# Sparse attention with two heads' transposes in one stage and one product tile, a planner clock that counts matmuls as traced, and a gate product moved by one place

## The chip, the core and the metric

The kernel runs on one core of one Trainium2 chip. The metric is device time in microseconds, the median of several runs of the same program. A core has a matrix engine (PE, TensorE), a vector engine (DVE), a scalar engine (ACT), GpSimd (POOL) and a queue processor (SP) that issues the memory transfers. Each engine executes its instructions in the order of the program, and semaphores tie the engines together.

## What is computed

Two blocks of a network are run, one behind the other, on 512 tokens of 1024 channels. The first has two layers. Each layer multiplies a normed x by a wide input matrix and feeds three mixers: an mLSTM (`ya`), sparse attention (`yb`) and differential attention (`yc`). Gates weigh the three results, an output matrix follows, and a gated feed-forward part ends the layer. The second block has an even layer (pooling and a spatial gate) and an odd layer (dilated attention and a gated convolution). The change lies in sparse attention, which per query takes the 128 best keys of an indexer:

```python
s = jnp.einsum('bqhd,bqkhd->bhqk', qb, k_sel).astype(f32) * (dh ** -0.5)
s = jnp.where(valid[:, None], s, -jnp.inf)
p = jax.nn.softmax(s, axis=-1).astype(v.dtype)
return jnp.einsum('bhqk,bqkhd->bqhd', p, v_sel)
...
merged = (gates[:, :, 0] * jnp.einsum('btc,cd->btd', y_a, w_branch[0])
          + gates[:, :, 1] * jnp.einsum('btc,cd->btd', y_b, w_branch[1])
          + gates[:, :, 2] * jnp.einsum('btc,cd->btd', y_c, w_branch[2]))
```

## The kernel before

**Tiling.** Tokens are four tiles of 128. A weight GEMM (`gemm`, line 352) accumulates products of 128x128 by up to 512 columns in PSUM tiles named `g`. Every f32 operand is split into two fp32r parts (`whi`, `wlo` of a weight on ACT and DVE; `xh`, `xl` of x), and three products stand for one. In the mixing part of a layer the weight GEMMs run in the order of the table `MIXING` (line 36): projections by name, `("gate", branch, half)` for gate products, `("br", b)` for branch products.

**Sparse attention** (`dsa`) is done by pair of heads (four pairs) and query tile i (four), 16 stages a layer. In the kernel before a stage computes the scores of both heads (`two_scores`: three matmuls a head, each on 64 rows of PE), takes softmax (DVE adds the bias and takes the maximum, ACT exponentiates), and then, head by head, transposes the probabilities (`probs_T`: matmuls against `ident` into a PSUM tile `t`, an ACT copy to `pt`), multiplies them by v into a `t` tile of its own, and scales the product into `y` on ACT. When a pair is through, `pair_over` stores y to the scratch `scr`. When all pairs are through, `load_y` fetches the pairs from `scr` to `tmp` and transposes them for the branch product `("br", 1)`, the last of a layer. The other two mixers do the same for their branches.

**The order of the work** is set while the program is written. The GEMM loop emits one k-step at a time and then calls `advance`, which lets waiting generators ("streams") emit their next step. Each keeps a time at which its inputs will be there. The time comes from a planner's clock: `count` (line 187) adds a cost per instruction to the clock of its engine, and the PE's clock is `now`. A transfer is counted as its bytes plus `LOAD`, 2100 ns. Buffers are counted too (`take`, `give`: two `pt`, two `t`, one set `yT` for the reload). The order on the chip is then fixed; what the planner counted wrongly turns into waits there. All instructions go through a wrapper and so carry line 62 in the profile; they are told apart by the names of their tiles.

**What the prediction touches**: `MIXING` (36), `LOAD` (45), the costs in `count` (187 to 216), `two_scores` (638), `probs_T` (657), `load_y` (668), `dsa` (721), and in `diff` the call of `probs_T`.

Of the kernel before, what the change touches and what calls it, by code (L numbers as in the profile page):

```python
# [10 lines left out]
FR = mybir.dt.float32r  # L11
AF = mybir.ActivationFunctionType
# [3 lines left out]
P = 128  # L16
# [16 lines left out]
POOLS = (2, 4, 8, 16)  # L33


MIXING = ("dq", "dv", "dk", "mo", "mq", "mv", ("gate", 2, 0), "mk", ("gate", 2, 1), "sk", "sv", "sq",
          ("gate", 0, 0), ("gate", 0, 1), ("br", 2), ("gate", 1, 0), ("br", 0), ("gate", 1, 1), ("br", 1))
BRANCHES = [item[1] for item in MIXING if item[0] == "br"]
FREE = "free"
# [84 lines left out]
class Net:  # L124
# [62 lines left out]
    def count(self, name, op, args):  # L187

        s = self.cur
        if name == "sync":  # L190
            self.t[name] = max(self.t[name], self.now) + 4 * math.prod(args[0].shape) / 360.0
            self.arrive = self.t[name] + LOAD
            if s:
                s.ready = max(s.ready, self.arrive)
            return
        n = max(math.prod(a.shape[1:]) for a in args if hasattr(a, "shape"))
        if op == "transpose":
            cost = 107.0
        elif name == "tensor":
            n = math.prod(args[0].shape[1:])  # L200
            cost = max(107.0, n / 2.4 + 3 if args[1].dtype == FR else 4 * n / 2.4)
        else:
            cost = {"vector": (60 + n) / 0.96, "scalar": (200 + n) / 1.4,
                    "gpsimd": 100.0 + n * (200 if op == "tensor_tensor" else 1)}[name]
        start = max(self.t[name], self.now)
        if s and s.last[0] not in (None, name) and op != "memset":
            start = max(start, s.last[1] + 60)
        self.t[name] = start + cost
        if s and op != "memset":
            s.last = (name, start + cost)  # L210
            s.ready = max(s.ready, start + cost + LAG)
        if name == "tensor":
            self.now = self.t[name]
# [206 lines left out]
    def rstd(self, ss, n, count):  # L420
        nc = self.nc
        ms = self.small(n)
        nc.vector.tensor_scalar(ms, ss, 1.0 / count, EPS, op0=OP.mult, op1=OP.add)
        r = self.small(n)
        nc.gpsimd.tensor_tensor(r, ms, self.nhalf[:, :n], op=OP.pow)
        return r
# [211 lines left out]
    def two_scores(self, w, qs, ks, i):  # L638

        ps = self.ps("s"), self.ps("s")  # L640
        ts = slice(i * P, (i + 1) * P)
        for n, (a, b) in enumerate(((0, 0), (0, 1), (1, 0))):
            for c in range(2):
                hp = slice(c * 64, c * 64 + 64)
                self.nc.tensor.matmul(ps[c][:, :w], qs[hp, a, ts], ks[hp, b, :w], start=(n == 0), stop=(n == 2))
        return ps

    def softmax(self, ps, w, bias, scale, total):
# [5 lines left out]
        nc.scalar.activation(s[:, :w], s[:, :w], AF.Exp, bias=m, scale=-1.0, accum_out=total)  # L654
        return s

    def probs_T(self, p, w):

        yield from self.take(pt=1, t=1)
        tr = self.transposed([p[:, j * P:(j + 1) * P] for j in range(w // P)])  # L660
        self.give("s")
        pt = self.buf("pt")
        self.nc.scalar.copy(pt[:, :w], tr[:, :w])
        self.give("t")
        yield
        return pt

    def load_y(self, scr, yT, pair):
# [52 lines left out]
    def dsa(self, q, k, v, bias, out):  # L721
        nc = self.nc
        heads = {}

        def part(pair, i):
            while pair not in heads:
                yield
            qs, ks, vn, y = heads[pair]
            w = (i + 1) * P
            yield from self.take(s=2, S=2)  # L730
            tot = self.small(2)
            pr = []
            for c, ps in enumerate(self.two_scores(w, qs, ks, i)):
                pr.append(self.softmax(ps, w, bias[i], 0.125, tot[:, c:c + 1]))
                self.give("S")
            yield
            r = self.small(2)
            nc.vector.reciprocal(r, tot)
            for c, p in enumerate(pr):
                hp = slice(c * 64, c * 64 + 64)  # L740
                pt = yield from self.probs_T(p, w)
                yield from self.take(t=1)
                yp = self.ps("t")
                for j in range(i + 1):
                    nc.tensor.matmul(yp[:, :64], pt[:, j * P:(j + 1) * P], vn[:, j, hp], start=(j == 0), stop=(j == i))
                self.give("pt")
                nc.scalar.activation(y[:, i, hp], yp[:, :64], AF.Copy, scale=r[:, c:c + 1])
                self.give("t")
                if c == 0:
                    yield  # L750
            if i == NT - 1:
                yield from self.pair_over(y, out, pair)

        yield from self.attend(lambda pair: self.pair_setup(heads, pair, q, k, v),
                               lambda pair: [part(pair, i) for i in range(NT)], 4)

    def attend(self, setup, parts, width):
# [9 lines left out]
    def diff(self, q, k, v, lamn, gout, out):  # L767
        nc = self.nc
        heads = {}

        def part(h, i):
            while h not in heads:
                yield
            qs, ks, vn, y = heads[h]
            w = (i + 1) * P
            yield from self.take(s=2, S=2)
            tot = self.small(2)
            pr = []
            for c, ps in enumerate(self.two_scores(w, qs, ks, i)):
                pr.append(self.softmax(ps, w, self.master[:, T - w:], 0.125, tot[:, c:c + 1]))  # L780
                self.give("S")
            yield
            r = self.small(2)
            nc.vector.reciprocal(r, tot)
            kap = self.small(1)
            nc.vector.tensor_scalar(kap, r[:, 1:2], tot[:, 0:1], lamn, op0=OP.mult, op1=OP.mult)
            nc.vector.scalar_tensor_tensor(pr[0][:, :w], pr[1][:, :w], kap, pr[0][:, :w], op0=OP.mult, op1=OP.add)
            self.give("s")
            yield
            pt = yield from self.probs_T(pr[0], w)  # L790
            yield from self.take(t=1)
            yp = self.ps("t")
            for j in range(i + 1):
                nc.tensor.matmul(yp[:, :P], pt[:, j * P:(j + 1) * P], vn[:, j, :], start=(j == 0), stop=(j == i))
            self.give("pt")
            nc.scalar.activation(y[:, i, :], yp[:, :P], AF.Copy, scale=r[:, 0:1])
            self.give("t")
            sq = self.buf("sq", (P, P))
            ss = self.small(1)
            nc.scalar.activation(sq, y[:, i, :], AF.Square, accum_out=ss)  # L800
            yield
            rr = self.rstd(ss, 1, P)
            yield
            nc.vector.scalar_tensor_tensor(y[:, i, :], y[:, i, :], rr, gout, op0=OP.mult, op1=OP.mult)
            if i == NT - 1:
                yield from self.pair_over(y, out, h)

        yield from self.attend(lambda h: self.pair_setup(heads, h, q, k, v),
                               lambda h: [part(h, i) for i in range(NT)], 4)


# [271 lines left out]
    def plan(self):  # L1083

        ins, want = self.ins, self.want
        for li in range(2):
# [4 lines left out]
            cols = {"dq": C_DQ, "dk": C_DK, "dv": C_DV, "mq": C_MQK, "mk": C_MQK + T, "mv": C_MV, "mo": C_MO, "sq": C_SQ}  # L1091
            for item in MIXING:
                if item in cols:
# [106 lines left out]
    def layer(self, li):  # L1200
# [152 lines left out]
        gates = {}  # L1353
        for item in MIXING:
            if item != "dq":
# [539 lines left out]
```

## Time and profile before

| | us |
|---|---|
| median of 3 runs | 3027.21 (3025.52 to 3029.02) |
| the profiled execution | 3023.1 |
| its span, first to last instruction | 3021.4 |
| PE busy | 2975.6 (98%) |
| DVE busy | 1572.8 (52%) |
| ACT busy | 1163.4 (39%) |
| POOL busy | 115.7 (4%) |

The profile's page gives busy time by engine, the chain of work that ended last, and the costliest groups of instructions. Other views of the same trace give each instruction in order of time, what an engine waited for, and the clock that was granted to PE. A matmul's record is longer than the distance to the next one, because matmuls are pipelined: distances are read from start times. A product in f32 makes two records, a transpose one.

### The profile page before, as it was taken

The page shows a single profiled execution, that of the slowest core. Times are in us where ns is not written, and L with a number is a line of the kernel's source. Part 1 is how long each engine was busy: PE and PEld are TensorE (multiplying, and loading weights), DVE is VectorE, ACT ScalarE, POOL GpSimd, SP SyncE. Part 2 cuts the span into 40 slices and gives each one's busy share as a digit, 9 for nine tenths or more (in the row PEclk, how much of TensorE's full clock was granted, in tenths as well). Part 3 has the DMA queues.
Part 4 walks back from the last instruction along what each step waited for, and adds up shares of the span by engine and source line. Part 5 has one row for each costly group of instructions (what it writes and reads, how often), then busy time and mean ns, then how long its engine had stood idle before and what let it go on. Part 6 is the DMA issues. An engine that isn't in the chain of part 4 may idle for free.

```text
span 3021.4 us, 38554 instructions
## 1 busy us (share of the span) xinstructions
PE 2975.6 (98%) x14474; PEld 2464.4 (82%) x14474; DVE 1572.8 (52%) x3018; ACT 1163.4 (39%) x2176; POOL 115.7 (4%) x128
## 2 busy tenths in 40 slices
PE   8999999999999999999999999999999999999999
PEld 6877887887888788888788888888888888888887
DVE  6888754544435788964444333444652233433534
ACT  4365454332323346545332223322333234444322
POOL 1100100000000110100000000000000000000000
PEclk9999999999999999999999999999999999999999
DMA  4545554535344344664434344424254433443534
GB/s 140 162 133 166 183 176 137 164 98 161 113 140 144 119 137 139 200 199 142 152 128 125 125 140 132 138 93 153 84 168 149 143 104 108 110 114 105 174 109 146
DMA packets 336023, 419.60 MB, mean 139 GB/s; under 512 B 37660, under 2 KB 167132, under 8 KB 335836
## 3 DMA queue, kind: packets, MB, share of 16 engines
q1 hardware_dynamic: 335836, 417.13, 44.0%
q8 instruction: 114, 1.87, 0.3%
q14 instruction: 73, 0.60, 0.1%
HBM read 339.37 MB, written 77.68 MB: 138 GB/s over the span
## 4 chain that ended last, share of the span: by engine, by line
PE 93%; DVE 3%; DMA 2%; ACT 1%; SPq 1%; issue 1%; POOL 0%; DVEq 0%; ACTq 0%; POOLq 0%
PE g L62 83%; PE t L62 6%; PE s L62 3%; DVE tmp L62 1%; DVE wlo L62 1%; SPq L62 1%; DMA wraw<-in_w_in_dram 1%; DVE small L62 0%; ACT whi L62 0%; DMA tmp<-scr 0%; DMA wraw<-in_w_gate_up_dram 0%; DMA scr<-tmp 0%; DMA pt<-in_norm_mix_g_dram 0%; DMA ld<-scr 0%; ACT tmp L62 0%
## 5 line engine op out<-in xcount | busy, mean ns | idle before, releaser
L62 DVE TENSOR_TENSOR wlo<-wraw,whi 128x1024 fp32r<-128x1024 f32 (+1 forms) x502 | 592.2, 1184 | 771.8 <-ACT whi L62 763.3
L62 PE MATMUL g<-xh,whi 128*128 128x512 f32 (+2 forms) x2256 | 889.1, 394 | 0.0
L62 PE MATMUL g<-xh,wlo 128*128 128x512 f32 (+2 forms) x2256 | 866.6, 384 | 0.0
L62 PE MATMUL g<-xl,whi 128*128 128x512 f32 (+2 forms) x2256 | 865.2, 383 | 0.0
L62 ACT ACTIVATE whi<-wraw 128x1024 fp32r<-128x1024 f32 (+1 forms) x502 | 513.5, 1027 | 802.7 <-PE g L62 686.4
L62 PEld LDWEIGHTS g<-xh,wlo 128*128 128x128 f32 (+1 forms) x2256 | 423.3, 188 | 86.1
L62 PEld LDWEIGHTS g<-xh,whi 128*128 128x128 f32 (+1 forms) x2256 | 423.8, 188 | 83.6 <-issue 6.1
L62 PEld LDWEIGHTS g<-xl,whi 128*128 128x128 f32 (+1 forms) x2256 | 424.3, 188 | 74.9
L62 PE MATMUL g<-whi,s 128*128 128x512 f32 x1536 | 480.0, 390 | 3.4 <-ACT tmp L62 3.4
L62 PEld LDWEIGHTS g<-whi,s 128*128 128x128 f32 x1536 | 288.4, 188 | 63.9 <-ACT tmp L62 4.5
L62 PE MATMUL g<-wlo,s 128*128 128x512 f32 x768 | 298.8, 389 | 0.0
L62 PE MATMUL g<-whi,xh 128*128 128x512 f32 x704 | 281.3, 400 | 0.0
L62 PE MATMUL g<-whi,xl 128*128 128x512 f32 x704 | 275.3, 391 | 0.6 <-DVE xl L62 0.6
L62 PE MATMUL g<-wlo,xh 128*128 128x512 f32 x704 | 275.3, 391 | 0.6 <-DVE wlo L62 0.6
L62 POOL TENSOR_TENSOR small<-small,nhalf 128x1 f32<-128x1 f32 (+2 forms) x108 | 110.1, 1021 | 2813.8 <-DVE small L62 2792.4
L62 PEld LDWEIGHTS g<-wlo,s 128*128 128x128 f32 x768 | 144.3, 188 | 29.3
L62 PEld LDWEIGHTS g<-whi,xh 128*128 128x128 f32 x704 | 132.7, 189 | 31.3 <-issue 3.7
L62 PEld LDWEIGHTS g<-whi,xl 128*128 128x128 f32 x704 | 132.6, 188 | 29.7 <-DVE xl L62 1.4
L62 PEld LDWEIGHTS g<-wlo,xh 128*128 128x128 f32 x704 | 132.9, 189 | 26.4 <-DVE wlo L62 1.0
L62 PE MATMUL g<-s,whi 128*128 128x512 f32 x416 | 135.6, 408 | 0.0
L62 ACT ACTIVATE tmp<-g 128x512 f32<-128x512 f32 (+1 forms) x108 | 62.9, 582 | 157.0 <-PE g L62 143.5
L62 DVE SCALAR_TENSOR_TENSOR tmp<-tmp,g 128x512 f32<-128x512 f32 x92 | 63.0, 685 | 97.2 <-ACT tmp L62 85.5
(199 smaller groups left out, 2594.3 us busy)
## 6 DMA issues: line engine op xcount, KB each, us to landing
wraw<-in_w_in_dram SPq DMA_DIRECT2D x120, 512.0 KB, 4.1
wraw<-in_w_gate_up_dram SPq DMA_DIRECT2D x88, 512.0 KB, 4.6
scr<-tmp SPq DMA_DIRECT2D x168, 256.0 KB, 2.8
wraw<-in_odd_w_in_dram SPq DMA_DIRECT2D x64, 512.0 KB, 3.7
ld<-scr SPq DMA_DIRECT2D x104, 256.0 KB, 5.4
wraw<-in_odd_w_in_dram SPq DMA_DIRECT2D x192, 128.0 KB, 2.3
wraw<-in_w_down_dram SPq DMA_DIRECT2D x44, 512.0 KB, 3.8
tmp<-scr SPq DMA_DIRECT2D x80, 256.0 KB, 5.2
```

The lines of the kernel that those rows point to most:

```text
L62: return f(*a, **kw)
```

## The change

- In `dsa` a stage transposes the probabilities of both heads (it takes both `pt` buffers for it), then, one step later, multiplies both and scales both. Both products go to halves of one PSUM tile, `yp[:, hp]`, where each had a tile of its own.
- `probs_T` becomes `transpose_probs`, without the step behind it and without taking `pt`; differential attention calls it with both written out, so that its stages are as before.
- The planner's cost of an fp32r product of n columns goes from n / 2.4 + 3 to (n + 32) / 2.4 ns (512 columns: 216.3 to 226.7), of an f32 product from 4n / 2.4 to no less than 214 ns (64 columns: 107 to 214). Of the two heads' score matmuls only the first is counted.
- In `MIXING` the gate product `("gate", 2, 1)` stands behind `sk` instead of ahead of it.

```diff
-MIXING = ("dq", "dv", "dk", "mo", "mq", "mv", ("gate", 2, 0), "mk", ("gate", 2, 1), "sk", "sv", "sq",
+MIXING = ("dq", "dv", "dk", "mo", "mq", "mv", ("gate", 2, 0), "mk", "sk", ("gate", 2, 1), "sv", "sq",
...
-            cost = max(107.0, n / 2.4 + 3 if args[1].dtype == FR else 4 * n / 2.4)
+            cost = max(110.0, (n + 32) / 2.4) if args[1].dtype == FR else max(214.0, 4 * n / 2.4)
...
-                self.nc.tensor.matmul(ps[c][:, :w], qs[hp, a, ts], ks[hp, b, :w], start=(n == 0), stop=(n == 2))
+                eng = self.nc.tensor if c == 0 else self.nc.tensor.eng
+                eng.matmul(ps[c][:, :w], qs[hp, a, ts], ks[hp, b, :w], start=(n == 0), stop=(n == 2))
...
-    def probs_T(self, p, w):
-
-        yield from self.take(pt=1, t=1)
+    def transpose_probs(self, p, w):
+
+        yield from self.take(t=1)
...
         self.give("t")
-        yield
         return pt
...
-            for c, p in enumerate(pr):
+            yield from self.take(pt=2)
+            pts = []
+            for p in pr:
+                pts.append((yield from self.transpose_probs(p, w)))
+            yield
+            yield from self.take(t=1)
+            yp = self.ps("t")
+            for c, pt in enumerate(pts):
                 hp = slice(c * 64, c * 64 + 64)
-                pt = yield from self.probs_T(p, w)
-                yield from self.take(t=1)
-                yp = self.ps("t")
                 for j in range(i + 1):
-                    nc.tensor.matmul(yp[:, :64], pt[:, j * P:(j + 1) * P], vn[:, j, hp], start=(j == 0), stop=(j == i))
+                    nc.tensor.matmul(yp[:, hp], pt[:, j * P:(j + 1) * P], vn[:, j, hp], start=(j == 0), stop=(j == i))
                 self.give("pt")
-                nc.scalar.activation(y[:, i, hp], yp[:, :64], AF.Copy, scale=r[:, c:c + 1])
-                self.give("t")
-                if c == 0:
-                    yield
+                nc.scalar.activation(y[:, i, hp], yp[:, hp], AF.Copy, scale=r[:, c:c + 1])
+            self.give("t")
...
-            pt = yield from self.probs_T(pr[0], w)
+            yield from self.take(pt=1)
+            pt = yield from self.transpose_probs(pr[0], w)
+            yield
```

PE has 13896 matmuls in both programs. The first place is PE in sparse attention of layer 0, last pair of heads, near its end. `s_` are probabilities, `pt_` their transposes, `ld_` v, `t_` PSUM tiles, `g_` a weight product; the numbers name single buffers, and in brackets stand the semaphores (by producer) that a row waits for. Before, with head 1 of query tile 2 and head 0 of tile 3:

```order
L62 MATMUL t_1355_5347<-ident_87,s_1328_5240 128x128 [waits Activation_49]
L62 MATMUL t_1355_5347<-ident_87,s_1328_5240 128x128 x2
L62 MATMUL t_1357_5353<-ident_87,s_1341_5286 128x128 [waits Activation_49]
L62 MATMUL t_1357_5353<-ident_87,s_1341_5286 128x128 x3
L62 MATMUL g_1293_5131<-xh_94,whi_1290_5118 128x512
L62 MATMUL g_1293_5131<-xl_95,whi_1290_5118 128x512
L62 MATMUL g_1293_5131<-xh_94,wlo_1291_5119 128x512
L62 MATMUL t_1359_5363<-ld_1260_4998,pt_1356_5351 128x64 [waits Activation_49]
L62 MATMUL t_1359_5363<-ld_1260_4998,pt_1356_5351 128x64 x2
L62 MATMUL t_1360_5368<-ld_1260_4998,pt_1358_5358 128x64 [waits Activation_49]
L62 MATMUL t_1360_5368<-ld_1260_4998,pt_1358_5358 128x64 x3
L62 MATMUL g_1317_5208<-xh_94,whi_1286_5102 128x512
```

And in the changed program, both heads of query tile 2:

```order
L62 MATMUL t_1308_5127<-ident_87,s_1289_5063 128x128 [waits PE_49]
L62 MATMUL t_1308_5127<-ident_87,s_1289_5063 128x128 x2
L62 MATMUL t_1310_5133<-ident_87,s_1291_5067 128x128 [waits Activation_49]
L62 MATMUL t_1310_5133<-ident_87,s_1291_5067 128x128 x2
L62 MATMUL g_1299_5091<-s4_1160_4595,whi_1213_4785 128x512
L62 MATMUL g_1299_5091<-s4_1161_4596,whi_1213_4785 128x512
L62 MATMUL g_1299_5091<-s4_1160_4595,wlo_1214_4786 128x512
L62 MATMUL t_1313_5144<-ld_1198_4730,pt_1309_5131 128x64 [waits Activation_49]
L62 MATMUL t_1313_5144<-ld_1198_4730,pt_1309_5131 128x64 x2
L62 MATMUL t_1313_5144<-ld_1198_4730,pt_1311_5137 128x64 [waits Activation_49]
L62 MATMUL t_1313_5144<-ld_1198_4730,pt_1311_5137 128x64 x2
L62 MATMUL g_1314_5153<-s4_1158_4593,whi_1211_4772 128x512
```

The two products that follow each other wrote two tiles (`t_1359`, `t_1360`) and now write one (`t_1313`); the GEMM around them was a gate product (`xh` by weights) and is now the branch product of the mLSTM (`s4` by weights).

The second place is PE where the output of sparse attention comes back (`tmp`, four pairs of heads) and is transposed. Before:

```order
L62 MATMUL g_1332_5257<-xh_94,wlo_1291_5119 128x512
L62 MATMUL t_1379_5441<-ident_87,tmp_1376_5435 128x128 x4
L62 MATMUL t_1381_5450<-ident_87,tmp_1377_5437 128x128 x4
L62 MATMUL t_1383_5459<-ident_87,tmp_1380_5448 128x128 x4
L62 MATMUL t_1384_5466<-ident_87,tmp_1382_5457 128x128 x4
L62 MATMUL g_1385_5473<-s4_1372_5431,whi_1345_5300 128x512
```

In the changed program, the first two of the four:

```order
L62 MATMUL g_1345_5315<-xh_94,wlo_1321_5191 128x512
L62 MATMUL t_1346_5322<-ident_87,tmp_1342_5300 128x128 x4
L62 MATMUL g_1345_5315<-xh_94,whi_1323_5205 128x512
L62 MATMUL g_1345_5315<-xl_95,whi_1323_5205 128x512
L62 MATMUL g_1345_5315<-xh_94,wlo_1324_5206 128x512
L62 MATMUL g_1345_5315<-xh_94,whi_1323_5205 128x512
L62 MATMUL g_1345_5315<-xl_95,whi_1323_5205 128x512
L62 MATMUL g_1345_5315<-xh_94,wlo_1324_5206 128x512
L62 MATMUL t_1348_5337<-ident_87,tmp_1344_5307 128x128 x4
L62 MATMUL g_1349_5344<-xh_94,whi_1320_5190 128x512
```

The transposes stood between the last gate product and the branch product; they now stand among the products of the last gate GEMM, 30 products behind the end of the branch product before it.

## Rows read from the trace of the kernel before

**Rows 1.** The page: busy time by engine, and the chain's shares by engine.

```profile
PE 2975.6 (98%) x14474; PEld 2464.4 (82%) x14474; DVE 1572.8 (52%) x3018; ACT 1163.4 (39%) x2176; POOL 115.7 (4%) x128
...
PE 93%; DVE 3%; DMA 2%; ACT 1%; SPq 1%; issue 1%; POOL 0%; DVEq 0%; ACTq 0%; POOLq 0%
```

**Rows 2.** Timeline in a gate GEMM: start us, us, engine, line, operation, out<-in, shape, count.

```profile
416.03 0.39 PE L62 MATMUL g<-xl,whi 128*128 128x512 f32 x1
...
416.26 0.40 PE L62 MATMUL g<-xh,wlo 128*128 128x512 f32 x1
```

**Rows 3.** What PE waited for: us in total, times, longest us.

```profile
PE t L62 <- DMA tmp<-scr: 14.5, 4, 6.0
...
PE g L62 <- ACT tmp L62: 3.4, 3, 1.7
PE t L62 <- DVE small L62: 2.4, 2, 1.7
...
PE s L62 <- ACT y L62: 0.5, 2, 0.3
```

**Rows 4.** Chain, ends of sparse attention, layers 0 and 1: start, us, what.

```profile
516.94 3.52 PE g L62 x15
...
531.62 3.43 PE g L62 x13
...
1463.26 3.52 PE g L62 x15
...
1477.92 6.21 PE g L62 x20
```

**Rows 5.** Timeline at the end of sparse attention, layer 0; idle before in brackets.

```profile
510.39 0.93 PE L62 MATMUL t<-ident,s 128*128 128x128 f32 x7
...
511.07 0.47 PE L62 MATMUL g<-xh,whi 128*128 128x512 f32 x1
...
522.06 1.06 SPq L62 DMA_DIRECT2D tmp<-scr  x2
...
526.34 1.99 PE L62 MATMUL t<-ident,tmp 128*128 128x128 f32 x8 [5.91 <-DMA tmp<-scr]
```

**Rows 6.** Windows: length, busy us by engine (count), granted clock share, DMA share, GB/s.

```profile
320.00:331.00 11.00, 9.27 (x41) 7.36 (x41) 8.76 (x27) 7.56 (x16) 2.64 (x2) 0.84 0.57 182
394.00:400.00 6.00, 5.75 (x37) 4.78 (x37) 2.77 (x11) 3.13 (x14) 0.00 (x0) 1.00 0.14 50
...
526.00:532.00 6.00, 4.32 (x18) 3.56 (x19) 1.95 (x3) 2.14 (x4) 0.00 (x0) 0.50 1.07 355
...
1472.00:1478.00 6.00, 3.99 (x17) 3.35 (x18) 1.66 (x3) 1.84 (x4) 0.00 (x0) 0.50 1.10 347
```

**Rows 7.** Timeline, products of two heads in a row, layer 0.

```profile
508.57 1.22 PE L62 MATMUL t<-ld,pt 128*128 128x64 f32 x10
```

**Rows 8.** Groups by shape: count, busy us, mean ns, idle before and releasers.

```profile
L62 ACT ACTIVATE whi<-wraw 128x1024 fp32r<-128x1024 f32 x432 | 455.2, 1058 | 711.6 <-PE g L62 599.4 <-DMA wraw<-in_w_gate_up_dram 42.3 <-DMA wraw<-in_w_in_dram 22.5
...
L62 ACT ACTIVATE y<-t,small 128x64 f32<-128x64 f32 x64 | 19.6, 312 | 31.4 <-PE t L62 30.4
```

**Rows 9.** Timeline around one product of sparse attention, layer 0.

```profile
410.00 0.37 ACT L62 COPY pt<-t 128x256 f32<-128x256 f32 x1 [0.71 <-PE t L62]
...
410.45 0.64 PE L62 MATMUL t<-ld,pt 128*128 128x64 f32 x4
...
410.93 0.50 PE L62 MATMUL t<-ident,s 128*128 128x128 f32 x3
411.13 0.31 ACT L62 ACTIVATE y<-t,small 128x64 f32<-128x64 f32 x1 [0.75 <-PE t L62]
```

**Rows 10.** The page's DMA issues: count, KB each, median us to landing.

```profile
tmp<-scr SPq DMA_DIRECT2D x80, 256.0 KB, 5.2
```

**Rows 11.** Timeline of PE, two stops in the mLSTM, layer 0.

```profile
323.18 0.39 PE L62 MATMUL t<-small,last 128*128 128x8 f32 x2 [1.71 <-DVE small L62]
...
395.55 0.62 PE L62 MATMUL s<-s,s 64*128 64x256 f32 x5 [0.26 <-ACT y L62]
```

## The prediction

> **What bounds the kernel now.** I read the page first. TensorE (PE) is busy for 98% of the span, 93% of the chain that ended last lies on it, and no other engine is busy for more than 52% [rows 1]. The 512-column products of the weight GEMMs ("g") start every 0.23 us (416.03, 416.26 [rows 2]). They, the transposes and the attention products fill PE, so an edit counts only if it changes the stops between PE's instructions or their spacing.
>
> Then PE's waits [rows 3]. They are few. The largest item is 14.5 us for `tmp<-scr`, four stops, at the two places where sparse attention ends: PE runs out of GEMM work, and the output of sparse attention has still to come back from memory before it can be transposed for the last branch product.
>
> The chain view shows the whole price [rows 4]. In layer 0 the last fifteen products that cover it end at 516.94 + 3.52 = 520.46, and the branch product starts at 531.62, 11.16 us later. The sixteen transposes between are needed anyway. At 0.10 us each (seven from 510.39 to 511.07 [rows 5]) they are 1.6 us, so 9.5 are lost. In layer 1 it is 1463.26 + 3.52 = 1466.78 to 1477.92, 11.14, so 9.5 again. Behind both stops PE stays slow for a while: the granted clock is 0.50 (1.2 GHz) from 526 to 532 and from 1472 to 1478 [rows 6]. The twenty products from 1477.92 take 6.21 us where 20 x 0.23 = 4.6 would do, the thirteen from 531.62 take 3.43 for 3.0 [rows 4]: 2.0 us more. Together 21.0 us.
>
> **The change part by part.** No instruction is added or removed. What changes is their order, and one dependency.
>
> *One product tile for two heads.* Before, each head's product had a tile of its own, and two heads that met ran without a stop: ten records in a row [rows 7], with ACT scaling behind them. Now both heads write halves of one tile, head 1's product stands straight behind head 0's, and its first matmul waits for ACT: the scaling of head 0, which reads that tile, has to come between. It is so in all 32 stages (4 pairs x 4 query blocks x 2 layers; 64 scalings of 128x64 [rows 8]). PE executes in order, so the GEMM products behind wait too. The price of a turn from one stretch [rows 9]: a product ends at 410.45 + 0.64 = 411.09, ACT starts at 411.13 and takes 0.31, to 411.44; from an ACT end (410.00 + 0.37 = 410.37) to the product that waited for it (410.45) pass 0.08, so PE goes on at 411.52. Without the wait its next work began at 410.93. That is 0.59 us a turn, 32 x 0.59 = **+18.9 us**. Ends: 0.43 (411.09 to 411.52, if the overlap with the product's own end were not lost), 13.8 us; and 0.8 if ACT is met in a 1.06-us weight conversion [rows 8] as often as its busy share of 39% says (0.39 x 0.53 = 0.2 more), 25.6 us. I take 0.59, since ACT's rows ahead of a scaling are the two copies, which end earlier.
>
> The Trainium skill (PSUM — Partial Sum Buffer, section "PSUM bank collisions raise a hardware error") asks that two engines be kept apart by bank and partition quadrant, not by address: disjoint columns don't help, and the new wait is what it asks for. No run here shows the contrary. If columns were enough, this term would be 0 and the sum 18.9 us lower.
>
> *Two transposes per stage.* The copies of both heads now follow each other on ACT, ahead of the products. Three GEMM products (0.7 us) lie between, as before; one copy took 0.37 us for 256 columns [rows 9]. The second copy has head 0's product and the turn as further cover. I take +1 us in all (0 to +4, an eighth of a microsecond a stage).
>
> *The program's clock, and the moved gate product.* The planner counts 226.7 ns for a 512-column product instead of 216.3, as the trace has it, and only one of the two score matmuls that start together. Sparse attention ends earlier against the GEMMs: its last product stands within branch 0, and 96 gate products follow before branch 1, with the reload's transposes among them. From the end of branch 0, which frees the tiles they go to, 30 products (6.8 us) cover what takes 1.6 us to issue (520.46 to 522.06) and 4.3 us more until the transposes start (526.34) [rows 4, 5]. The other three loads have more. So the 21.0 us go but for about 0.7 a layer: **-19.6 us**. The least is -12, if the loads land late behind the weight loads in SP's queue and each layer still waits 4.5 us.
>
> *The other reloads.* Branches 2 and 0 fetch theirs in the same way, and the planner counts 2.1 us for any load (LOAD = 2100), where `tmp<-scr` takes 5.2 us to land [rows 10]. Before, PE waited for none of them: all four stops are at the end. With a shorter cover a stop of up to 3.1 us is possible at the first load of each, four places. I take 1.25 at each, **+5 us** (0 to +12).
>
> *All other re-weaving.* Every step is placed a twentieth fewer products behind what it waits for (216.3/226.7), in differential attention, the mLSTM, the odd layer and at the GEMMs' PSUM tiles. Where cover was just enough PE stops now. Before, such stops cost 3.4 + 2.4 + 0.5 = 6.3 us [rows 3]; they can vanish or double, -6 to +6, and I take **+4**, since covers shrink everywhere. The moved gate product is in this term: it and `sk` change places whole, with their loads.
>
> Sum: 18.9 + 1 - 19.6 + 5 + 4 = **+9.3 us** on the profiled run's 3023.1 us, 3032.4. The median of the runs is 4.1 us above the profiled one: 3027.2 + 9.3 = **3036**.
>
> **Rivals**, as medians; 0.2% (6 us) is about what a measurement of this kernel tells from no change.
>
> *Gain and loss cancel.* The turns cost their lower end and re-weaving nothing: 13.8 + 1 - 19.6 + 5 = 0, 3027. For: the two large terms are of one size and opposite sign. Against: 0.59 is read off neighbouring rows. 28%.
>
> *Faster.* The turn is covered, because head 1's product would have waited for its own copy anyway, and only what exceeds that wait counts. At 0.1 us a turn: 3.2 + 1 - 19.6 + 5 + 4 = -6.4, 3021; the sign turns at 0.30. For: both copies go through ACT, one behind the other. Against: three GEMM products and head 0's product lie between. 5%.
>
> *The clock falls.* Behind a stop of 1.71 us at 323.18 [rows 11] the granted clock was 0.84 over 11 us [rows 6], 0.16 x 11 = 1.8 us lost. If each turn lost half of this, 32 x 0.9 = 29 us: 3065. Against: in 394 to 400, with a short stop at 395.55 [rows 11], the clock stayed at 1.00 [rows 6]. 5%.
>
> The Trainium skill (TensorE: Matmul & The Clock Gate, section "A second HAM failure mode: psum-queue depth-cycling") tells of a kernel in which short idle times at each change of PSUM buffer made the clock fall and rise again. Here the short stop left it at full speed, which is why I give the case no more.
>
> *ACT in the way.* If a weight conversion stands ahead of head 0's scaling in every third turn: 11 x 1.06 = 12 us more, 3048. 10%.
>
> *The tail stays.* If SP's queue holds the reloads back behind weight loads, a stop of 4.5 us a layer stays: 8 us more, 3044. 5%.
>
> **How the numbers follow.** The forecast of +9 has 47%; its own range is +3 to +15 (3030 to 3042), from the bounds of the re-weaving. The rivals take 28, 5, 5, 10 and 5%. The range that should hold the time 8 times in 10 reaches down to the case in which gain and loss cancel (3026) and up to the busy ACT (3048); it leaves out the fallen clock, the faster case and an edge of the cancelling one. Slower by over 0.2%: 0.66 (46 of the forecast's 47, and the three costly rivals' 20); within 0.2%: 0.28; faster: 0.06, the faster rival and one part in a hundred of the forecast.
>
> **What would show it.** Right: PE's waits list about 32 stops at product tiles with ACT `y` as releaser, each about 0.3 us of idle as that view counts; no 6-us stop for `tmp<-scr`; a granted clock above 0.9 behind the end of sparse attention. Wrong: no such stops (the turn is covered), a stop at the end of sparse attention as before, or a granted clock under 0.9 within it. If the stops are there and the time is the same, the re-weaving gave back what I took it to cost.

## The result and the profile after

The changed kernel takes 3046.68 us (median of 4, 3045.11 to 3048.88) against 3026.36 for the kernel before (4 runs): 1.0069 times the time, 95% interval 1.0052 to 1.0087, or 20 us more. The forecast was slower by 9, 3036, in a range of 3026 to 3048. Side and range held; the size was less than half of what came.

The page of the changed kernel gives the span and the busy times, as [rows 1] do for the kernel before:

```profile
span 3047.1 us, 38595 instructions
PE 2989.6 (98%) x14474; PEld 2463.3 (81%) x14474; DVE 1575.2 (52%) x3018; ACT 1163.1 (38%) x2176; POOL 121.2 (4%) x128
```

Work and shares are nearly the same; the span is 25.7 us longer than the profiled one before, where the medians differ by 20. The two profiled executions lie towards opposite ends of their runs (3023.1 us before, 3048.88 now), so some 5 us in what follows are spread between runs. What PE waited for in the changed kernel (us in total, times, longest), as [rows 3]:

```profile
PE t L62 <- DVE tmp L62: 16.2, 11, 11.8
PE t L62 <- ACT y L62: 13.7, 32, 0.8
PE g L62 <- ACT tmp L62: 5.2, 4, 2.2
PE g L62 <- DVE wlo L62: 3.9, 2, 2.8
PE t L62 <- DMA tmp<-scr: 3.6, 2, 3.1
...
PE t L62 <- ACT pt L62: 0.9, 3, 0.3
```

There are 32 stops of a product on ACT `y`, one a stage. The stops at `tmp<-scr` fell from 14.5 us in four to 3.6 in two: the longer (3.1) is at a reload ahead of sparse attention, the other (0.5) at its end in layer 1. And the waits of the GEMMs for ACT `tmp` and DVE `wlo` grew from 4.0 us (3.4 and 0.6) to 9.1. One turn in the timeline (start us, us, engine, line, operation, out<-in, shape, count, idle before in brackets):

```profile
401.84 0.55 PE L62 MATMUL t<-ld,pt 128*128 128x64 f32 x4
...
402.43 0.31 ACT L62 ACTIVATE y<-t,small 128x64 f32<-128x64 f32 x1 [0.61 <-PE t L62]
...
402.80 0.66 PE L62 MATMUL t<-ld,pt 128*128 128x64 f32 x4 [0.41 <-ACT y L62]
```

Head 0's product ends at 402.39, ACT scales it from 402.43 to 402.74, head 1's product starts at 402.80. Windows of the changed kernel (columns as in [rows 6]), the first over sparse attention, the others where the kernel before had just stopped:

```profile
400.00:450.00 50.00, 46.04 (x280) 37.26 (x278) 20.75 (x54) 23.82 (x61) 0.00 (x0) 1.00 0.48 144
526.00:532.00 6.00, 6.00 (x32) 5.02 (x31) 3.83 (x4) 2.93 (x5) 0.00 (x0) 1.00 0.48 156
1472.00:1478.00 6.00, 6.00 (x28) 4.98 (x27) 3.81 (x6) 2.12 (x2) 0.00 (x0) 1.00 0.02 6
```

PE is busy throughout the last two at a granted clock of 1.00, where [rows 6] have 0.50. So both large terms of the sum are there. What is new is in the middle of the mixing part, ahead of sparse attention. PE in layer 0, and below it what DVE did until then:

```profile
290.23 0.50 PE L62 MATMUL g<-xh,wlo 128*128 128x512 f32 x1 [2.81 <-DVE wlo L62]
```

```profile
286.90 1.42 DVE L62 TENSOR_TENSOR tmp<-tmp,lay 128x512 f32<-128x512 f32 x2
288.35 0.69 DVE L62 TENSOR_TENSOR tmp<-tmp,tmp 128x512 f32<-128x512 f32 x1
288.95 1.22 DVE L62 TENSOR_TENSOR wlo<-wraw,whi 128x1024 fp32r<-128x1024 f32 x1
```

DVE works without a pause on normalisations; the part of a weight that PE needs next stands behind them. This one stop comes with the moved gate product and not with the new costs: gate_moved_only and no_clock, below, have a stop of 2.8 us for `wlo` in each layer under the planner's old costs. Other stops of the changed kernel are not in those two, among them the two longest of layer 1:

```profile
1236.95 0.79 PE L62 MATMUL g<-xh,whi 128*128 128x512 f32 x1 [2.23 <-ACT tmp L62]
...
1265.29 1.09 PE L62 MATMUL t<-ident,tmp 128*128 128x128 f32 x4 [3.11 <-DMA tmp<-scr]
```

At all three the granted clock falls to 0.50 for a few microseconds, as these windows of the changed kernel show. The kernel before has one such fall ahead of sparse attention, behind its stop at 323 us [rows 6]:

```profile
290.00:300.00 10.00, 9.77 (x36) 7.92 (x37) 9.30 (x18) 3.12 (x4) 0.00 (x0) 0.83 0.83 259
1230.00:1245.00 15.00, 12.11 (x47) 9.38 (x46) 14.65 (x28) 7.44 (x13) 4.95 (x3) 0.89 0.63 206
1260.00:1275.00 15.00, 11.89 (x50) 9.80 (x49) 7.10 (x20) 7.38 (x17) 0.00 (x0) 0.77 0.85 284
```

Counted as in the prediction, 0.17 x 10 + 0.11 x 15 + 0.23 x 15 = 6.8 us are lost so, where the kernel before loses 1.8. By this estimate 5 us of the loss ahead of sparse attention are the clock.

**Where the time is.** To add it up I took, for each PE record, the distance from its start to the next start, less the usual distance of that kind of record (the lower quartile over all records of that kind in both traces). This excess is summed over three stretches, cut at the same amount of work in every kernel: both layers between the early projections and sparse attention (123 to 386 and 977 to 1334 us in the kernel before), sparse attention with its end (386 to 547, 1334 to 1501), and the rest. Turns are products that stand over 0.4 us too far behind another product.

| kernel | ahead of sparse attention | sparse attention and end | of it turns | rest | sum |
|---|---|---|---|---|---|
| before | 49.3 | 52.7 | 0 | 35.2 | 137.2 |
| changed | 71.2 | 49.3 | 18.9 (32) | 42.6 | 163.1 |
| both_first | 69.2 | 33.1 | 0 | 39.4 | 141.6 |
| heads_only | 50.9 | 54.1 | 19.1 (32) | 35.8 | 140.8 |
| clock_only | 67.7 | 32.5 | 0 | 39.5 | 139.7 |
| fp32r_cost_only | 66.6 | 32.1 | 0 | 40.8 | 139.5 |
| gate_moved_only | 50.9 | 49.1 | 0 | 33.8 | 133.8 |
| no_clock | 51.4 | 52.9 | 19.7 (32) | 36.9 | 141.1 |
| gate_back | 67.9 | 53.0 | 19.3 (32) | 39.5 | 160.4 |
| both_first_alone | 51.2 | 46.9 | 0 | 36.8 | 134.9 |
| both_first_no_clock | 50.8 | 35.2 | 0 | 33.8 | 119.8 |
| costs_lag200 | 60.3 | 36.8 | 0 | 33.2 | 130.4 |
| best_lag200 | 54.9 | 33.0 | 0 | 33.1 | 121.0 |
| all_costs | 67.3 | 127.8 | 0 | 43.4 | 238.5 |

The second column stands near 50 in every kernel with the planner's old costs, and near 67 or above in every one with the new PE costs (60 with a longer margin, below). The third, all_costs apart, stands near 33 where there are neither turns nor a stop at the end, and near 50 where there is one of the two. Kernels that differ in sparse attention alone share the order of the work ahead of it, so the second column holds four different orders under the new costs and three under the old: enough to tell them apart, not enough to exclude chance in the size.

### The profile page after: what moved, and what is told of

The parts are those of the page before. It is cut to its first block, busy times and chain, and to the rows that moved or that the text cites. A ratio compares the mean times of both kernels' runs of the same rounds, so it can differ in the third digit from the quotient of the medians.

```text
span 3047.1 us, 38595 instructions
## 1 busy us (share of the span) xinstructions
PE 2989.6 (98%) x14474; PEld 2463.3 (81%) x14474; DVE 1575.2 (52%) x3018; ACT 1163.1 (38%) x2176; POOL 121.2 (4%) x128
## 4 chain that ended last, share of the span: by engine, by line
PE 59%; DVE 1%; ACT 1%; DMA 1%; issue 1%; POOL 0%; SPq 0%; DVEq 0%; ACTq 0%; POOLq 0%
PE g L62 53%; PE t L62 4%; PE s L62 2%; DVE tmp L62 1%; ACT s L62 0%; DMA tmp<-scr 0%; DVE wlo L62 0%; DMA s<-xd 0%; DVE small L62 0%; DVE s L62 0%; ACT y L62 0%; ACT pt L62 0%; ACT whi L62 0%; POOL small L62 0%; DVE tk L62 0%
## 5 line engine op out<-in xcount | busy, mean ns | idle before, releaser
L62 POOL TENSOR_TENSOR small<-small,nhalf 128x1 f32<-128x1 f32 (+2 forms) x108 | 116.5, 1081 | 2830.7 <-DVE small L62 2805.3
L62 PEld LDWEIGHTS t<-ld,pt 128*128 128x128 f32 x720 | 96.3, 190 | 30.2 <-ACT y L62 18.1
```

Source lines behind the costliest of these rows:

```text
L62: return f(*a, **kw)
```

## The experiments

Each ratio is to runs of the kernel before on the same chip, with its 95% interval.

**both_first**: the turn alone.

```diff
             for c, pt in enumerate(pts):
...
                 self.give("pt")
-                nc.scalar.activation(y[:, i, hp], yp[:, hp], AF.Copy, scale=r[:, c:c + 1])
+            for c, hp in enumerate(hps):
+                nc.scalar.activation(y[:, i, hp], yp[:, hp], AF.Copy, scale=r[:, c:c + 1])
             self.give("t")
```

> The changed kernel, but both heads' products are written into their halves of the tile first, and both scalings by ACT follow behind them; nothing then makes head 1's product wait for ACT. Theory of the turn (PE, ACT, PE inside a stage: 32 stops of 0.57 us and more, as PE's starts in the changed kernel have it, 20.9 us over the nominal spacing of the products): about 3046.7 - 19 = 3028 us, and the list of PE's waits no longer has the 32 stops of a product on ACT `y`. Rival, the turn is only where a stage waits anyway (for its copies, or for ACT): the stops come back as waits on ACT `pt`, and the time stays within 5 us of 3046.

3028.95 us, 1.0006 (0.9996 to 1.0016): 17.7 less than the changed kernel. The same stage of this kernel:

```profile
402.07 1.00 PE L62 MATMUL t<-ld,pt 128*128 128x64 f32 x8
403.10 0.52 ACT L62 ACTIVATE y<-t,small 128x64 f32<-128x64 f32 x2 [1.05 <-PE t L62]
```

Both products run in one piece and both scalings follow. PE's waits for ACT `y` are gone, and those for ACT `pt` sum to 0.6 us in two stops: nothing took the turn's place. Some is lost again at reloads (`tmp<-scr`: 8.2 us in four stops, the longest, 4.9, ahead of sparse attention in layer 1; the changed kernel has 3.6).

**heads_only, clock_only, gate_moved_only**: each edit alone, on the kernel before. heads_only is the hunks of the change in `probs_T`, `dsa` and `diff`; the other two are

```diff
-            cost = max(107.0, n / 2.4 + 3 if args[1].dtype == FR else 4 * n / 2.4)
+            cost = max(110.0, (n + 32) / 2.4) if args[1].dtype == FR else max(214.0, 4 * n / 2.4)
...
-                self.nc.tensor.matmul(ps[c][:, :w], qs[hp, a, ts], ks[hp, b, :w], start=(n == 0), stop=(n == 2))
+                eng = self.nc.tensor if c == 0 else self.nc.tensor.eng
+                eng.matmul(ps[c][:, :w], qs[hp, a, ts], ks[hp, b, :w], start=(n == 0), stop=(n == 2))
```

```diff
-MIXING = ("dq", "dv", "dk", "mo", "mq", "mv", ("gate", 2, 0), "mk", ("gate", 2, 1), "sk", "sv", "sq",
+MIXING = ("dq", "dv", "dk", "mo", "mq", "mv", ("gate", 2, 0), "mk", "sk", ("gate", 2, 1), "sv", "sq",
```

> The kernel before with the edit of sparse attention alone (two transposes a stage, both products in one tile); the planner's costs and the order of the weight products are those of before. If the turn is a cost of the tile alone: the same 32 stops, + 18 to 21 us, and the stop at the end of sparse attention stays (two layers of about 10 us): 3045 to 3048. If the edit by itself lets sparse attention end earlier and so takes the stops at the end away: 3026 + 19 - 20 = 3026, and what makes the changed kernel slow lies in the other two edits.

> The kernel before with the planner's costs alone (512-column product 226.7 ns instead of 216.3, f32 product no less than 214, one of two score matmuls counted). As I argued, the clock takes the stops at the end of sparse attention away (21 us) and re-weaving gives some of it back (9 us): about 3014. If the stops that the changed kernel has in the middle of a mixing part (271 to 290 us and 1109 to 1265 us; the re-weaving cost about 29 us there and elsewhere and not 9) come from the clock, they are here too: 3026 - 22 + 29 = 3033. If the end of sparse attention was moved by the pairing of heads and not by the clock: the stop of 6 us at `tmp<-scr` stays, and 3026 or more.

> The kernel before with the gate product of branch 2, second half, behind the GEMM `sk` instead of ahead of it, and nothing else. In the prediction it cost nothing of its own: 3026 within 4 us. Rival: it is the cause of the stops on ACT `tmp` and DVE `wlo` in the middle of the mixing part, because the gate's evacuation then meets DVE while it is at the selection of keys and at the normalisation of `sk`: + 8 us in layer 0 and more in layer 1, 3036 to 3042, with stops of 1 to 3 us near 271 to 290 us.

heads_only takes 3027.14, 1.0000 (0.9990 to 1.0009); clock_only 3025.58, 0.9993 (0.9984 to 1.0003); gate_moved_only 3021.57, 0.9982 (0.9973 to 0.9991). No edit alone makes the kernel slower, and together they cost 20 us. PE's waits in heads_only say how its zero comes about:

```profile
PE t L62 <- ACT y L62: 13.8, 32, 0.8
...
PE t L62 <- DMA tmp<-scr: 1.1, 1, 1.1
```

The turns are there, the stops at the end are not, with the old costs in the planner. clock_only has no stop of 6 us at the end either (its longest for `tmp<-scr` is 2.7), and no turns; the gain went into the stretch ahead of sparse attention, 49.3 to 67.7. So the first two edits each win the end, which can be won once; the heads' edit pays for it with turns, the costs with stops in the middle. With both, both prices are paid. My second expectation for clock_only (3033) summed these right but for the size.

gate_moved_only contradicts the rival that I gave it. It removes the stops on ACT `tmp` and DVE `small` near 297 and 323 us ([rows 11] have the second), and brings others, here in its waits:

```profile
PE g L62 <- DVE wlo L62: 6.3, 3, 2.8
```

With them the second column is 1.6 us higher than before. What it gains lies in the two other columns (3.6 and 1.4 us), and why is not settled.

The mechanism of clock_only's middle is seen at one step, the transposes of `md` in the mLSTM. PE's row and DVE's last `md` row ahead of it, in the kernel before:

```profile
305.25 0.28 DVE L62 SCALAR_TENSOR_TENSOR md<-s,md 128x128 f32<-128x128 f32 x1
...
308.31 0.60 PE L62 MATMUL t<-ident,md 128*128 128x128 f32 x4
```

In clock_only, PE and the first `md` row:

```profile
309.61 0.28 DVE L62 SCALAR_TENSOR_TENSOR md<-s,md 128x128 f32<-128x128 f32 x1
...
310.00 1.09 PE L62 MATMUL t<-ident,md 128*128 128x128 f32 x4 [5.42 <-issue]
```

Before, PE came 2.8 us after DVE had ended (305.53 to 308.31). With the new costs the same transposes stand where PE arrives at 304.6, five microseconds ahead of DVE's first row, and it waits; the profile names no releaser (`issue`), but PE goes on 0.11 us after the end of that row (309.89). On PE 1402 records stand ahead of the step instead of 1437, 35 fewer, about 8 us at 0.23 us each; on DVE 585 instructions instead of 579. That is far more than a twentieth of its cover of 2.8 us: shifts of the steps ahead of it have added up. The changed kernel has the same step behind 1429 records, 1.3 us behind DVE's last row (313.34 to 314.68), and doesn't stop there; its stops are at the other steps shown above, and how each of them arose was not followed.

**fp32r_cost_only**: the first half of the cost line alone.

```diff
-            cost = max(107.0, n / 2.4 + 3 if args[1].dtype == FR else 4 * n / 2.4)
+            cost = max(110.0, (n + 32) / 2.4) if args[1].dtype == FR else 4 * n / 2.4
```

> The kernel before with one of the three planner edits: the cost of an fp32r product, (n + 32) / 2.4 instead of n / 2.4 + 3. If the rate of the GEMM products alone makes steps come too early (the stops in the middle) and lets sparse attention end earlier (no stop at the end): 3025, as clock_only. If the stops in the middle come from the other two (f32 products counted double, half of the score products not counted), which shift attention against the GEMMs within a stage: 3010 to 3015 if the end is still freed, 3026 if not.

3025.51, 0.9992 (0.9983 to 1.0002), and in the table a copy of clock_only. The 5% on the GEMM products does it all; the f32 and score costs do nothing that shows.

**no_clock and gate_back**: the changed kernel with one part undone, the planner's costs (the diff of clock_only reversed) or the table `MIXING`.

> The changed kernel with the planner's costs of before: pairing of heads in one tile and the moved gate product remain. Alone, the heads' edit took 20 us of turns and gave the 20 us of the stops at the end back (3027), the moved gate product gave 5 us (3021.6), the costs alone gave the same 20 us of the end and took as many in the middle (3025.6). Theory (the end can be given back only once, so together the costs bring nothing and their stops in the middle remain): without the costs 3027 - 5 = 3022, up to 3027. Rival (the loss of the changed kernel comes from the heads and the gate product meeting each other): it stays at 3040 or more.

> The changed kernel with the gate product of branch 2 back ahead of `sk`; pairing in one tile and the new costs remain. Alone the moved product gave 5 us (3021.6 against 3026.6), beside the heads' edit 1.6 (3025.5 against 3027.1). If that holds beside the new costs: 3046.7 + 2 to 5 = 3049 to 3052. Rival: with the new costs the moved product meets DVE where it is latest (stops of 1.0, 1.2, 1.6 and 3.0 us between 271 and 290 us in the changed kernel), and without it 5 to 7 us a layer come back: 3033 to 3040.

no_clock takes 3025.51, 0.9995 (0.9985 to 1.0004), 21 us less than the changed kernel: its middle is at 51.4. gate_back takes 3046.23, 1.0061 (1.0046 to 1.0076), no different from the changed kernel. Neither of my values for it came: beside the new costs the moved product gives nothing and costs nothing.

**both_first_no_clock and both_first_alone**: two transposes a stage without turns, with the planner's old costs, with and without the moved gate product.

> Two heads' products into one tile, both before the scalings, the moved gate product, and the planner's costs of before. If the three findings add (no turn: - 18 to - 20 against the same kernel with the turns; the stops at the end gone by the pairing; no stops from the costs): 3003 to 3008, below both kernels. If without the turns sparse attention runs further ahead and its reloads meet PE again (in both_first there were 8.2 us of waits for `tmp<-scr`, in heads_only 1.1): 3010 to 3016.

> The kernel before with the heads' edit alone in the form without turns (both products first, then both scalings). Against heads_only (3027.1) it lacks only the turns: - 18 to - 20, 3007 to 3009. If the gate product's 5 us are counted fully in the best version (3007.6, which has it): 3009 to 3013. If the 20 us of the end come back without the turns, since sparse attention's place against the GEMMs is another: 3020 or more.

both_first_no_clock takes **3007.63 us, 0.9933 (0.9918 to 0.9948)**, 20 us less than the kernel before (3027.3 beside it) and 39 less than the changed one. Its PE waits:

```profile
PE g L62 <- DVE wlo L62: 6.3, 3, 2.8
...
PE t L62 <- DMA tmp<-scr: 1.7, 4, 0.9
```

both_first_alone takes 3018.05, 0.9967 (0.9955 to 0.9979), between my second and third value. The stop at the end is back in it (`tmp<-scr`: 12.3 us in two stops), though heads_only, which differs by the order inside a stage and so a little in the weaving, has none. The chain of both_first_alone at the end of layer 0 (start, us, what):

```profile
519.39 1.06 ACT whi L62
...
520.48 1.24 DVE wlo L62
...
521.73 0.38 SPq L62
...
522.17 4.57 DMA tmp<-scr
...
526.87 1.94 PE t L62 x8
```

The last two reloads stand in SP's queue behind a weight load, which waits for a buffer that DVE frees at 521.72. In heads_only the two last reloads are behind weight loads too and go out later, at 524.96, but all are transposed among GEMM products: 33 stand between the last product of sparse attention and the first transposes, and 21 between the second and the third reload's, where both_first_alone has 27 and none. So the end seems to hang on how many GEMM products are left and on the place of a weight load in SP's queue. The planner moves both, and no run here moves one without the other.

**all_costs and costs_lag200**: why correcting one clock brings stops. In all_costs the durations of DVE and ACT are corrected as well; in costs_lag200 only a margin is added, both on top of the diff of clock_only.

```diff
-            cost = {"vector": (60 + n) / 0.96, "scalar": (200 + n) / 1.4,
+            cost = {"vector": (145 + n) / 0.96, "scalar": max(310.0, (115 + n) / 1.07),
```

```diff
-LAG = 100.0
+LAG = 200.0
```

> The kernel before with the planner's PE costs of the change and, besides, DVE and ACT costs near the traced durations (DVE, 512 elements: 596 to 684 ns, traced 0.68 to 0.69; ACT, 512: 509 to 586, traced 0.58 to 0.60; 1024: 874 to 1064, traced 1.06; ACT never under 310). Theory of the proportions: in the planner before, all engines were counted too fast by a like share; with PE alone corrected, steps that wait for DVE or ACT are placed too early against the products, and that is where the stops of clock_only in the middle come from. Then about 3026 - 20 + 5 = 3011. Rival (the stops come from a PE clock that is right but from transfers counted at 2.1 us, or from mere re-weaving): 3020 to 3030, as clock_only.

> The kernel before with the planner's PE costs of the change and LAG 200 instead of 100 ns, the margin that it leaves between the end of a step and the next one that needs it, without slowing any engine in the plan. If the stops of clock_only in the middle (about 20 us) come from steps that stand too close behind what they wait for, a longer margin takes half of them or more away, and sparse attention still ends before the GEMMs do: 3008 to 3016. If it spills behind the GEMMs, as with all costs raised (3123.7): 3035 or more. If the stops are re-weaving by chance: 3020 to 3030.

all_costs takes 3123.7, 1.0316 (1.0301 to 1.0332): the expectation was off by 113 us. Its second column is no lower, 67.3, and sparse attention no longer fits beside the GEMMs. Between 515 and 575 us of its trace no GEMM product stands on PE:

```profile
515.00:575.00 60.00, 49.88 (x223) 40.81 (x223) 11.72 (x47) 26.99 (x81) 0.00 (x0) 0.54 0.16 49
```

PE runs attention alone, a sixth of the time idle, at a granted clock of 0.54. The theory that truer costs all round would mend it has fallen.

costs_lag200 takes 3016.07, 0.9959 (0.9944 to 0.9974), 9.5 us less than clock_only, at the upper edge (3016) of what I had set for steps that stand too close. The `md` transposes in it:

```profile
308.41 0.29 DVE L62 SCALAR_TENSOR_TENSOR md<-s,md 128x128 f32<-128x128 f32 x1
...
309.76 0.60 PE L62 MATMUL t<-ident,md 128*128 128x128 f32 x4
```

PE comes 1.1 us behind DVE and doesn't wait. The second column falls from 67.7 to 60.3; about 11 us of the 18 that the costs had brought remain, so the margin took less than the half that I expected. The rest fell by 6.3 us beside it, and the third column rose by 4.3.

**best_lag200**: both_first_no_clock with that margin.

> The best version so far (both products before the scalings, the moved gate product, the planner's costs of before: 3007.6) with LAG 200 instead of 100 ns. It has few stops left in the middle (two of 3.0 us at DVE `wlo`, 0.9 to 1.7 at others; about 20 in small ones against the GEMMs' spacing). If the margin helps there as I think: 3000 to 3005. If sparse attention then ends too late: a stop for `tmp<-scr` at the end again, 3010 to 3025.

3008.42, 0.9940 (0.9924 to 0.9957): no change against both_first_no_clock, and between my two values. With the old costs the margin buys nothing.

## Why the prediction was right in its side and short in its size

*The turns.* Right. 0.59 us each and 18.9 in all were forecast; the 32 turns sum to 18.9 us of excess in the changed kernel (most are 0.57, the longest 1.01), and taking them away saved 17.7 us (both_first) and 17.9 (no_clock to both_first_no_clock). Neither rival on the turn came: it was not covered, and ACT was never in a weight conversion for long (longest wait 0.8). The Trainium skill (PSUM — Partial Sum Buffer, section "PSUM bank collisions raise a hardware error") was read as asking for this turn. It forbids two engines to touch one bank and quadrant at the same time, and so ACT to read while PE writes there; both products before both scalings keep to it for nothing. That columns of one tile might be enough was not tried.

*The second copies.* Right: PE waited 0.9 us for ACT `pt`, against +1.

*The end of sparse attention.* Right in size (about 20 us; without its turns the changed kernel has 49.3 - 18.9 = 30.4 in that stretch, before 52.7), wrong in cause. I laid it to the planner's clock alone. The heads' edit does it too (heads_only), and without the turns it loses it again (both_first_alone).

*The other reloads.* +5 forecast; the changed kernel has one stop of 3.1 us there, as long as the longest that I thought possible.

*The re-weaving.* This is the step that failed: +4, with bounds of -6 and +6. Turns 18.9, all else in the stretch of sparse attention -22.3 (the copies are in it) and the other reload 3.1 make about nothing of the 26 us by which the sums of the table differ. So 26 us are re-weaving, 21 by the medians: the rise ahead of sparse attention (21.9) and in the rest (7.4), less that reload. It comes from the planner's new cost of a GEMM product: with the old costs 19.8 of the 21.9 are gone (no_clock, 51.4), and that cost alone brings 17.3 (fp32r_cost_only, 66.6). I sized the term by stops that the kernel before had (6.3 us; I left out 13.7 for DVE `tmp`, of which 11.9 is one stop near the program's start). But the old stops say nothing of how much cover stood behind the steps without a stop. The step to take was to read, at each step that waits for DVE or ACT, how long PE came after its input (2.8 us at `md`), and what a 5% shift adds up to (35 records at `md`) along a chain in which DVE is busy 44.82 of 50 us, as in this window of the kernel before:

```profile
250.00:300.00 50.00, 48.16 (x233) 39.93 (x232) 44.82 (x92) 26.86 (x48) 5.14 (x5) 1.00 0.61 195
```

*The clock's fall* (5%) did not come at the turns: the granted clock is 1.00 over 400 to 450, with seven of them in it. The Trainium skill (TensorE: Matmul & The Clock Gate, section "A second HAM failure mode: psum-queue depth-cycling") tells of short idle times that made the clock swing; turns of this length don't here. It fell at the stops of 2.2 to 3.1 us ahead of sparse attention, at a cost of about 5 us more than before (estimated above), for which I had no term.

*Gain and loss cancel* (28%) holds for heads_only, 3027, though its turns cost the middle value and not the lower end: 19 against 18 (54.1 - 19.1 = 35.0 in that stretch, before 52.7). That the other edits would each take their own 20 us for the same end was not among the cases. The time lay inside the range by luck: the upper bound was put there for a busy ACT, which was not the cause.

What stays open: why the moved gate product is worth 5 us alone, nothing beside the new costs, and 10 in both_first_no_clock (there most of it is the stop at the end: 46.9 to 35.2); and which steps hold the part of the re-weaving that a longer margin doesn't remove.

## What to carry to other kernels

Two heads may share a PSUM tile if all products into it come before the first reading of it; one read in between costs a turn through two engines per stage, and here that was 18.9 us of a gain of 22.3. Two edits that remove the same stop add up to one gain and two prices, so each is to be timed alone and the sum not taken. In an order that is planned by counted times, an error that is corrected on one engine alone can use up the slack that the error had given, and correcting all of them can push work out of its cover; the slack behind each step is to be read from the trace first.

## What was not expected of the hardware

In all_costs the granted clock is 1.00 in 510 to 516 us and 0.50 (1.2 GHz, the lower of its two levels) in 516 to 562. The last GEMM product had ended at 510.70, and the fall came within a stop of PE:

```profile
516.47 1.12 PE L62 MATMUL t<-ident,s 128*128 128x128 f32 x4 [2.22 <-ACT y L62]
```

Over 515 to 575 us, 0.54 on the mean, PE was busy for 49.88 of the 60 us with small f32 products, scores and transposes. In the changed kernel 46.04 busy us of 50, with GEMM products between short stops, kept 1.00. What in the two stretches makes the difference no run here separates.
